# A row of inverse roots sent to all partitions through DRAM instead of by transposes

## The chip, the core and the metric

The kernel runs on one core of a Trainium2 chip. The metric is the device time of one execution in microseconds, as the median of several runs. The core has five engines that run their own instruction streams: TensorE (PE, matmuls and transposes), VectorE (DVE), ScalarE (ACT), GpSimd (POOL) and SyncE (SP, which issues most DMAs; ACT issues the others). Every stream is worked off in order, and an instruction that has to wait holds back all that stand behind it in its stream.

## The reference

One decoder layer over 2048 tokens of width 1024. `h = RMSNorm(x)` is projected by one wide matrix, the result is cut into three branches (an RWKV-7 time mixing, a sliding-window attention, a cross-attention), each branch is gated and projected back, the three are merged by sigmoid gates, and the merged row is projected by `w_out` and added to `x`. The change touches the first line alone:

```
def rms_norm(x, g):
    xf = x.astype(jnp.float32)
    y = xf * lax.rsqrt(jnp.mean(xf * xf, axis=-1, keepdims=True) + RMS_EPS)
    return (y * g.astype(jnp.float32)).astype(x.dtype)
...
h = rms_norm(x, norm_g[l])
p = h @ w_in[l]
```

## The kernel before

The tokens are worked off in four superblocks of 512 (`TB`). Activations lie transposed, channels on the partitions and 512 tokens along the row, and every float32 product is made of three matmuls on a high and a low half (`gemm3`, L534 to L536; in the output product L1334 to L1336). So `h` of a superblock is eight pairs of tiles `hH`, `hL` of 128 x 512.

To scale `x` by its inverse root, the kernel needs one factor for each token, as a row of 512, the same on all 128 partitions. The sums of squares come the other way, with tokens on partitions. While superblock `sb` is worked on, `x_sums(sb + 1, ss)` (L1350) loads eight blocks of the next tokens through ACT's DMA queue and squares and sums them on ACT. `x_scales(sb + 1, ss)` (L1360) adds the two halves on DVE (L1366, tile `rs`, 128 x 4), takes the power -0.5 on POOL (`rpow`, L489 and L491), spreads each column over 128 columns on DVE (`bcast_T`, L572), transposes the four 128 x 128 pieces on PE (L574) into a PSUM tile `as_`, and copies that on ACT (L1371) to the tile `rb`, which is one of the six buffers `rt`. `x_cols` (L1374) loads eight blocks of the transposed `x` through ACT's DMA queue (L1380), multiplies each by `rb` on DVE (L1383), and splits it into `hH` (ACT, L1385) and `hL` (DVE, L1386).

This stands at the end of each of the first three superblocks, here called the first, second and third end (at about 520, 1041 and 1561 us of the profile). At that place PE works on eight merges (`merge(0, ...)`, twelve matmuls each, into one of two PSUM tiles `mm`), and then on the output product (`output`, L1327), which begins at about 531.6, 1052.6 and 1573.5 us. A merge's PSUM tile is read by DVE at L1317, the result is added at L1318, and `split_acc` splits it (ACT L1322, DVE L1324). The output product fills four PSUM tiles: the first `mm`, `as_`, the second `mm`, `as_`. Its first `mm` is the tile of the seventh merge, its second that of the eighth, so each waits for that merge's L1317.

The weights come as blocks of 128 x 512 in high and low halves, tile `whl`, seven buffers (`WR`). A block is either loaded as `raw` (L514, three buffers) and split on ACT (L515) and DVE (L516), sometimes kept in DRAM for later (L520), or read back from there (L511). All of these DMAs stand in SP's stream.

The order within the streams is not that of the code. `order` (L310) gives all instructions to `lay_out` (L196), which plays the program through with costs from a table (`cost_PE` and so on) and fixes every engine's order. A plain DMA counts 2200 ns there (`cost_SP`, L142). What is planned later, by the framework, are the semaphores: the DMAs of SP and ACT share eight of them, DMAHW0 to DMAHW7, in turn, and a DMA that is to count on one of them first waits, in its own engine's stream, until the DMA that last used it has landed.

Of the kernel before, what the change touches and what calls it, by code (L numbers as in the profile page):

```python
# [9 lines left out]
F32 = mybir.dt.float32  # L10
# [10 lines left out]
TB = 512  # L21
# [297 lines left out]
def build(tc, A, nsb=4):  # L319
    nc = tc.nc  # L320
# [3 lines left out]
    def pool(name, bufs, **kw):  # L324
        return es.enter_context(tc.tile_pool(name=name, bufs=bufs, **kw))
# [24 lines left out]
    def s_ps():  # L350
        return ps.tile([128, 512], F32, name="as_", bufs=2)
# [43 lines left out]
    def tmp(tag="rt", bufs=NRT):  # L395
        return rp.tile([128, TB], F32, name=tag, bufs=bufs)
# [55 lines left out]
    def pcol(name, i=0):  # L452
        o, w = PV[name]
        return pv[:, o + i:o + i + 1]
# [13 lines left out]
    def dcol(name, i=0):  # L468
        return dv[:, DV[name][0] + i:DV[name][0] + i + 1]
# [14 lines left out]
    def rpow(out, in_, add, scale=1.0):  # L484

        if scale == 1.0:
            G.tensor_scalar(out, in_, add, None, op0=ALU.add)  # L487
        else:
            G.tensor_scalar(out, in_, scale, add, op0=ALU.mult, op1=ALU.add)  # L489
        n = out.shape[-1]  # L490
        G.tensor_tensor(out, out, mhalf[:, :n], op=ALU.pow)  # L491


    dp = pool("dp", 1, space=bass.MemoryType.DRAM)
# [44 lines left out]
    def proj(blk, hT, n=TB):  # L539
        o = mm_ps()  # L540
        gemm3(o[:, :n], [(w, (hT[0][:, k, :n], hT[1][:, k, :n])) for k, w in enumerate(wtiles(A["w_in"][blk], 8, ("in", blk)))])
        return o
# [25 lines left out]
    def bcast_T(out, st, nh, ntile):  # L568

        w = 128 // nh  # L570
        rep = tmp()[:, :ntile * 128]
        V.tensor_copy(rep.rearrange("p (a b) -> p a b", b=w), st[:, :ntile * nh].unsqueeze(2).to_broadcast([128, ntile * nh, w]))  # L572
        for i in range(ntile):
            PE.transpose(out[:, i * 128:(i + 1) * 128], rep[:, i * 128:(i + 1) * 128], ident)  # L574
# [69 lines left out]
    def row_sums(rows):  # L644

        ss = xp.tile([128, 4, 2], F32, name="ss", bufs=2)
        for i, xr in enumerate(rows):
            sq = rp.tile([128, 512], BF16, name="ibc", bufs=2)
            if i % 2:
                V.tensor_tensor_reduce(sq, xr, xr, 1.0, 0.0, ALU.mult, ALU.add, ss[:, i // 2, 1:])  # L650
            else:
                S.activation(sq, xr, AF.Square, accum_out=ss[:, i // 2, :1])
        rs = xp.tile([128, 4], F32, name="rs", bufs=2)
        n = len(rows) // 2
        V.tensor_tensor(rs[:, :n], ss[:, :n, 0], ss[:, :n, 1], op=ALU.add)
        return rs
# [80 lines left out]
    def shift(o, blk, mu, omu, sb, tag, bufs=1, t=None):  # L737
        t = rp.tile([128, TB], F32, name=tag, bufs=bufs) if t is None else t
        S.activation(t, o, AF.Copy, scale=omu)
        V.scalar_tensor_tensor(t[:, 1:], o[:, :TB - 1], mu, t[:, 1:], op0=ALU.mult, op1=ALU.add)  # L740
        V.scalar_tensor_tensor(t[:, 0:1], carry[sb % 2][:, blk:blk + 1], mu, t[:, 0:1], op0=ALU.mult, op1=ALU.add)
        V.tensor_copy(carry[1 - sb % 2][:, blk:blk + 1], o[:, TB - 1:TB])  # L742
        return t
# [6 lines left out]
    def park(sb):  # L750

        return [[dp.tile([4, 128, 4, 2, 128], F32, name=f"{n}{sb}_{u}") for u in range(2)] for n in ("fq", "fb")] + \
            [[dp.tile([4, 64, 4, 2, C], F32, name=f"fv{sb}_{u}") for u in range(2)]]
# [307 lines left out]
    def split_y(y, yh, yl, br, j, sb):  # L1061
        a = yp.tile([128, TB], F32R, name="yh")
        b = yp.tile([128, TB], F32R, name="yl")
        S.activation(a, y, AF.Copy)
        V.tensor_tensor(b, y, a.bitcast(F32), op=ALU.subtract)  # L1065
        yh.append(a)
        yl.append(b)
# [231 lines left out]
    def gate(i, o, hT):  # L1299
        gp = proj(B_G + 8 * i + o, hT)  # L1300
        t = gp_.tile([128, TB], F32, name="gt", bufs=2) if i else g2()
        S.activation(t, gp, AF.Tanh, scale=0.5)  # L1302
        return t
# [46 lines left out]
    def x_sums(sb, ss):  # L1350

        for i in range(4):
            for u in range(2):
                yield 45
                xr = gp_.tile([128, 512], F32, name="sx", bufs=1)
                load = nc.scalar.dma_start(xr, A["x"][sb * TB + i * 128:sb * TB + (i + 1) * 128, u * 512:(u + 1) * 512])
                manual[load.ins.name] = [newest[0]]
                S.activation(xr, xr, AF.Square, accum_out=ss[:, i, u:u + 1])

    def x_scales(sb, ss=None):  # L1360

        if not sb:
            rs = row_sums(x0)
        else:
            rs = xp.tile([128, 4], F32, name="rs", bufs=2)
            V.tensor_tensor(rs, ss[:, :, 0], ss[:, :, 1], op=ALU.add)  # L1366
        rpow(rs, rs, EPS, 1.0 / D)
        bc = s_ps()
        bcast_T(bc, rs, 1, 4)
        rb = tmp()  # L1370
        S.activation(rb, bc, AF.Copy)  # L1371
        return rb
# [17 lines left out]
    for i, _ in enumerate(mem_kv(mT)):  # L1390
        if i == AT1:
            rb = x_scales(0)
# [3 lines left out]
    for sb in range(nsb):  # L1396
        wa = proj(B_WA, hT)
        low = shift(wa, B_WA, pcol("mu_wa"), dcol("omu_wa"), sb, "rr_")
        S.activation(low[EV], low[EV], AF.Tanh)

        lwla = [rp.tile([128, TB], F32R, name=f"lwla{i}") for i in range(2)]
        for t, h, o in zip(lwla, (EV, OD), (OD, EV)):
            S.activation(t[h], low[h], AF.Copy)
            V.tensor_tensor(t[o], low[h], t[h].bitcast(F32), op=ALU.subtract)
        yas = []
        ya, yb, yc_ = ([], []), ([], []), ([], [])
        accs = []

        def stream_r():
            parks = park(sb)  # L1410
            dk = xp.tile([128, 4, NC_], F32, name="dk", bufs=1)
            Pl = xp.tile([128, 4, NC_], F32, name="Pl", bufs=1)
            yts = []
            for p0 in (0, 2):
                group = []
                fn, fy = (dp.tile([4, 2, NC_, 32, 32], F32, name=f"{n}{sb}_{p0}") for n in ("fn", "fy"))
                for p in (p0, p0 + 1):
                    yield from rwkv_prep(p, p - p0, parks, dk, Pl, fn, sb, hT, lwla, group)
                yield from rwkv_inverse(group, parks, fn, fy)
                yts += [g[2] for g in group]  # L1420
            yield from rwkv_chain(parks, dk, Pl, hT, yts, yas)
            yield 0.412

        def stream_f():
            for h in range(4):
                yield from cross_head(h, sb, hT, *yc_)
            if not sb:
                rope_tables(0)
            yield from swa_kv(sb, hT)
            yield 6.938  # L1430
            for j in range(4):
                yield from weave(swa_pair(j, sb, hT, *yb), merge(2, *yc_, accs, hT, first=True, orange=(2 * j, 2 * j + 1)))
            yield from merge(1, *yb, accs, hT)
            for o in range(8):
                gates.append(gate(0, o, hT))
                yield 5.908

        gates = []
        ss = xp.tile([128, 4, 2], F32, name="ss", bufs=2)
        streams = [paced(g, PACE[min(sb, 1)][i]) for i, g in enumerate((stream_r(), stream_f()))]  # L1440
        if sb + 1 < nsb:
            streams.append(x_sums(sb + 1, ss))
        for _ in weave(*streams):
            pass
        for p in range(4):
            split_y(yas[p], *ya, "a", p, sb)
        rb = None
        if sb + 1 < nsb:
            rope_tables(sb + 1)
            rb = x_scales(sb + 1, ss)  # L1450
        parts = []
        for o in range(8):
            for _ in merge(0, *ya, accs, hT, gates=gates, orange=(o,)):
                pass
            parts.append(split_acc(accs[o]))
        if rb is not None:
            hT = x_cols(sb + 1, rb)
        output(sb, *zip(*parts))
# [4 lines left out]
def paced(g, paces):  # L1463

    for f, d in zip(paces, g):
        yield f * d


def weave(*gens):

    live = [[0.0, i, g] for i, g in enumerate(gens)]
    now = 0.0
    while live:
        live.sort(key=lambda x: x[:2])
        e = live[0]
        try:
            d = next(e[2])
        except StopIteration:
            live.pop(0)
            continue  # L1480
        e[0] += d
        t = min(x[0] for x in live)
        if t > now:
            yield t - now
            now = t
# [64 lines left out]
```

## Time and profile before

| what | value |
|---|---|
| median of 3 runs | 2143.12 us (2143.11 to 2143.8) |
| the profiled execution's own time | 2143.2 us |
| its span, first to last instruction | 2141.4 us |
| PE busy | 2125.9 us, 14260 matmuls and transposes |
| DVE, ACT, POOL busy | 1418.5, 802.1, 133.6 us |
| mean granted TensorE clock | 1.000 |
| DMA | 519.17 MB, mean 242 GB/s |

In rows of the timeline the first number is the start in us of the span, the second the duration in us; then come the engine, the line, the operation and what it writes and reads. SPq and ACTq are DMAs issued by these engines, and their duration is the time of the issue, not of the transfer. In rows by line and window, "DMA to landing" is the time from the start of the issue to the last piece's arrival. A matmul of 512 columns shows about 0.39 us but follows the one before it after some 0.23 us, as they are pipelined.

### The profile page before, as it was taken

Reading aid. Unit: us, or ns where it says so; the run is one execution under the profiler, and the core shown is the slowest. Engines: PE = TensorE matmul, PEld = TensorE weight load, DVE = VectorE, ACT = ScalarE, POOL = GpSimd, SP = SyncE. Lnnn points to the kernel's source line nnn. Section 1 sums busy time; section 2 is a strip of 40 time slices with the busy share of each in tenths; the row PEclk is TensorE's granted clock in tenths of the full one; section 3 lists DMA queues with packets and bytes.
Section 4 is the critical chain, followed back from the end, with each engine's and each line's share of the span. In section 5 each row is a group of like instructions: output and inputs, shape, how many; then the busy total and the mean of one; then the engine's idle time right before and its main releaser. Section 6 shows DMA issues by size and latency. Waiting matters only on the chain.

```text
span 2141.4 us, 37426 instructions
## 1 busy us (share of the span) xinstructions
PE 2125.9 (99%) x14260; PEld 1753.8 (82%) x14260; DVE 1418.5 (66%) x3234; ACT 802.1 (37%) x1699; POOL 133.6 (6%) x180
## 2 busy tenths in 40 slices
PE   9999999999999999999999999999999999999999
PEld 7888887778888888878888888887888888888787
DVE  7879888468576787546647778736455777873532
ACT  7655554326344353303424434420423334331220
POOL 1001000001001000001000000000100010000000
PEclk9999999999999999999999999999999999999999
DMA  9988888987866678695876667777676676768665
GB/s 331 364 282 271 272 289 283 340 294 251 285 203 205 192 218 239 198 311 193 281 254 211 201 180 228 236 231 260 216 264 220 197 204 199 233 186 269 217 206 181
DMA packets 308594, 519.17 MB, mean 242 GB/s; under 512 B 89280, under 2 KB 175552, under 8 KB 308416
## 3 DMA queue, kind: packets, MB, share of 16 engines
q1 hardware_dynamic: 292288, 487.42, 70.9%
q10 hardware_dynamic: 16128, 29.37, 4.2%
q8 instruction: 113, 1.85, 0.4%
q14 instruction: 65, 0.53, 0.1%
HBM read 378.80 MB, written 137.89 MB: 241 GB/s over the span
## 4 chain that ended last, share of the span: by engine, by line
PE 91%; DVE 4%; DMA 3%; ACT 1%; issue 1%; POOL 0%; SPq 0%; ACTq 0%; DVEq 0%; POOLq 0%
PE mm L534 23%; PE mm L535 23%; PE mm L536 23%; PE mm L1334 1%; PE mm L1336 1%; PE mm L1335 1%; DMA raw<-in_w_in 1%; PE rw L1016 1%; PE rw L999 1%; PE oo L1283 1%; DVE whl L516 1%; PE rw L831 1%; PE rw L850 1%; DMA k<-whl 1%; PE oo L831 1%
## 5 line engine op out<-in xcount | busy, mean ns | idle before, releaser
L534 PE MATMUL mm<-hH,whl 128*128 128x512 f32 x1888 | 745.2, 395 | 2.0 <-DVE carry L742 1.4
L535 PE MATMUL mm<-hL,whl 128*128 128x512 f32 x1888 | 743.5, 394 | 0.0
L536 PE MATMUL mm<-hH,whl 128*128 128x512 f32 x1888 | 742.5, 393 | 0.0
L534 PEld LDWEIGHTS mm<-hH,whl 128*128 128x128 f32 x1888 | 354.8, 188 | 74.4 <-ACT whl L515 1.8
L536 PEld LDWEIGHTS mm<-hH,whl 128*128 128x128 f32 x1888 | 354.7, 188 | 71.4
L535 PEld LDWEIGHTS mm<-hL,whl 128*128 128x128 f32 x1888 | 355.0, 188 | 70.1 <-DVE hL L1386 0.2
L515 ACT ACTIVATE whl<-raw 128x512 fp32r<-128x512 f32 x174 | 109.1, 630 | 186.4 <-PE mm L536 131.7
L516 DVE TENSOR_TENSOR whl<-raw,whl 128x512 fp32r<-128x512 f32 x174 | 119.2, 687 | 61.7 <-ACT whl L515 55.7
L534 PE MATMUL mm<-yh,whl 128*128 128x512 f32 x384 | 151.4, 394 | 1.3 <-DVE gt L1317 1.2
L535 PE MATMUL mm<-yl,whl 128*128 128x512 f32 x384 | 150.3, 391 | 0.0
L536 PE MATMUL mm<-yh,whl 128*128 128x512 f32 x384 | 149.7, 390 | 0.0
L1302 ACT ACTIVATE gt<-mm 128x512 f32<-128x512 f32 x64 | 37.8, 590 | 179.3 <-PE mm L536 179.0
L534 PEld LDWEIGHTS mm<-yh,whl 128*128 128x128 f32 x384 | 72.1, 188 | 17.2 <-DVE gt L1317 1.6
L1317 DVE SCALAR_TENSOR_TENSOR gt<-gt,mm 128x512 f32<-128x512 f32 x32 | 21.9, 686 | 95.5 <-PE mm L536 95.3
L535 PEld LDWEIGHTS mm<-yl,whl 128*128 128x128 f32 x384 | 72.1, 188 | 15.0 <-DVE yl L1065 0.5
L536 PEld LDWEIGHTS mm<-yh,whl 128*128 128x128 f32 x384 | 72.1, 188 | 14.7
L487 POOL TENSOR_SCALAR st<-st 128x4 f32<-128x4 f32 (+1 forms) x32 | 12.7, 397 | 1019.7 <-DVE st L1093 418.8
L1341 DVE SCALAR_TENSOR_TENSOR ya<-mm,ya 128x512 f32<-128x512 f32 x16 | 11.0, 689 | 93.8 <-PE mm L1336 93.8
L1251 ACT ACTIVATE g<-g,mxs,st 128x128 f32<-128x128 f32 x128 | 61.6, 484 | 28.1 <-DVE mxs L1244 28.1
L892 DVE TENSOR_TENSOR ibc<-km,Yi 128x126 f32<-128x126 f32 (+22 forms) x248 | 62.9, 254 | 7.7 <-DMA km<-fn 2.1
L893 DVE TENSOR_TENSOR Yi<-Yi,ibc 128x126 f32<-128x126 f32 (+22 forms) x248 | 62.7, 253 | 5.6
L491 POOL TENSOR_TENSOR st<-st,mhalf 128x8 f32<-128x8 f32 (+1 forms) x36 | 52.7, 1463 | 3.0
(1828 smaller groups left out, 3579.5 us busy)
## 6 DMA issues: line engine op xcount, KB each, us to landing
whl<-k SPq DMA_DIRECT2D x474, 512.0 KB, 4.2
k<-whl SPq DMA_DIRECT2D x162, 512.0 KB, 4.8
raw<-in_w_in SPq DMA_DIRECT2D x118, 256.0 KB, 4.2
fq<-big SPq DMA_DIRECT2D x64, 256.0 KB, 4.4
fb<-big SPq DMA_DIRECT2D x64, 256.0 KB, 4.3
big<-fq SPq DMA_DIRECT2D x32, 512.0 KB, 6.4
big<-fb SPq DMA_DIRECT2D x32, 512.0 KB, 5.6
ya<-in_x ACTq DMA_DIRECT2D x32, 256.0 KB, 4.7
```

Source lines behind the costliest of these rows:

```text
L491: G.tensor_tensor(out, out, mhalf[:, :n], op=ALU.pow)
L515: S.activation(w[:, 0], raw, AF.Copy)
L516: V.tensor_tensor(w[:, 1], raw, w[:, 0].bitcast(F32), op=ALU.subtract)
L534: PE.matmul(out, lh, rh, start=i == 0, stop=False)
L535: PE.matmul(out, lh, rl, start=False, stop=False)
L536: newest[0] = PE.matmul(out, ll, rh, start=False, stop=i == n - 1).ins.name
L831: m = PE.matmul(g[:, c], BK[h, c0 + c], Q[h, c0 + c], start=True, stop=True)
L892: V.tensor_tensor(bc[:, :m, :w], Nb[:, s, s + 1:].unsqueeze(1).to_broadcast([128, m, w]), B[:, :m, s:s + 1].to_broadcast([128, m, w]), op= ...
L893: V.tensor_tensor(B[:, :m, s + 1:], B[:, :m, s + 1:], bc[:, :m, :w], op=ALU.add)
L1251: S.activation(P_, P_, AF.Exp, scale=r2[:, b, i:i + 1], bias=mx[:, b, i:i + 1], accum_out=mx[:, b, 2 + i:3 + i])
L1302: S.activation(t, gp, AF.Tanh, scale=0.5)
L1317: V.scalar_tensor_tensor(g, g, 1.0, pp, op0=ALU.add, op1=ALU.mult)
```

## The change

For the second to the fourth superblock, `x_scales` now ends after the power. It writes the 128 x 4 tile `rs` to a row of 512 numbers in DRAM (tile `xr`, one for each superblock), so that each partition's four numbers go to four places 128 numbers apart: 512 pieces of 4 bytes. It is called by the third of the woven streams, right after the last sum of squares. After `rope_tables`, one DMA reads the row back to all 128 partitions of an `rt` buffer (128 pieces of 2 KB). The spreading on DVE (L572), the four transposes (L574) and ACT's copy (L1371) are gone at the three ends; the first superblock keeps them. Both new DMAs are in SP's stream.

```
         rpow(rs, rs, EPS, 1.0 / D)
+        if sb:
+            row = dp.tile([1, TB], F32, name=f"xr{sb}")
+            nc.sync.dma_start(row[0].rearrange("(i t) -> t i", t=128), rs)
+            return row
         bc = s_ps()
...
+        rows = []
+
+        def stream_x():
+            yield from x_sums(sb + 1, ss)
+            rows.append(x_scales(sb + 1, ss))
+
         if sb + 1 < nsb:
-            streams.append(x_sums(sb + 1, ss))
+            streams.append(stream_x())
...
             rope_tables(sb + 1)
-            rb = x_scales(sb + 1, ss)
+            rb = tmp()
+            nc.sync.dma_start(rb, rows[0].to_broadcast([128, TB]))
```

In the changed file the lines below L1367 stand 4 lower up to the streams and 10 lower after the reading DMA's place: L1380, L1383, L1385 and L1386 of before are L1384, L1387, L1389 and L1390, the write is L1370, the read L1461. The planner orders the new program anew; PE, DVE, ACT and SP differ from before at the three ends only.

SP's stream at the second end, changed kernel, with the semaphores that each instruction waits for (`DMAHW` and a number: that semaphore's last DMA; the first name in a DMA's row is mostly the semaphore that it counts on itself):

```order
L511 DMA whl_11453<-k143_6205 128x1024 [waits DMAHW7_49,PE_49]
L1370 DMA xr2_11140<-rs_11136 128x4x1 [waits DMAHW0_49,Pool_49]
L514 DMA raw_11587<-in_w_out 128x512 [waits DMAHW1_49,DVE_49]
L1461 DMA rt_11184<-xr2_11140 128x512 [waits DMAHW2_49,DMAHW0_49]
L520 DMA k155_11472<-whl_11467 128x1024 [waits DMAHW4_49]
L511 DMA whl_11486<-k144_6241 128x1024 [waits DMAHW7_49,PE_49]
```

The write counts on DMAHW0, a load of `w_out` behind it on DMAHW1, and the read waits for the write by DMAHW0. Before, L511, L514, L520 and L511 followed each other there.

ACT's stream at the same place, before:

```order
L515 ACTIVATE whl_11477<-raw_11478 128x512 [waits DMAHW3_49,DMAHW4_49,DMAHW0_49,PE_49]
L1371 ACTIVATE rt_11194<-as__11187 128x512 [waits PE_49]
L1380 DMA rt_11386<-in_xt 128x512
L1380 DMA rt_11391<-in_xt 128x512 [waits DMAHW0_49]
L1380 DMA rt_11396<-in_xt 128x512 [waits DMAHW2_49]
L1322 ACTIVATE g2_11307<-mB_8942 128x512 [waits DVE_49]
L1380 DMA rt_11401<-in_xt 128x512 [waits DMAHW4_49]
L1380 DMA rt_11406<-in_xt 128x512 [waits DMAHW5_49]
L1322 ACTIVATE g2_11333<-mB_9093 128x512 [waits DVE_49]
```

and in the changed kernel:

```order
L515 ACTIVATE whl_11467<-raw_11468 128x512 [waits DMAHW5_49,DMAHW6_49,DMAHW2_49,PE_49]
L1384 DMA rt_11376<-in_xt 128x512 [waits DMAHW3_49]
L1384 DMA rt_11381<-in_xt 128x512 [waits DMAHW5_49]
L1384 DMA rt_11386<-in_xt 128x512 [waits DMAHW6_49]
L1384 DMA rt_11391<-in_xt 128x512 [waits DMAHW0_49]
L1384 DMA rt_11396<-in_xt 128x512 [waits DMAHW1_49]
L1322 ACTIVATE g2_11297<-mB_8937 128x512 [waits DVE_49]
L1322 ACTIVATE g2_11323<-mB_9088 128x512 [waits DVE_49]
```

All five loads of `xt` now stand ahead of both splits L1322. The fourth waits for DMAHW0, whose last DMA is the write of the row, and the fifth for DMAHW1, whose last DMA is the load of `raw_11587` in SP's rows above. Before, the five waited for DMAs issued by 1041.44 us: the fifth for the `whl` load of that time.

DVE's stream at the second end, changed kernel (`mm_11308`, `mm_11329` and `mm_11355` are the sixth, seventh and eighth merge):

```order
L1317 SCALAR_TENSOR_TENSOR g2_11069<-g2_11069,mm_11308 128x512 [waits PE_49]
L1324 TENSOR_TENSOR mB_11299<-mB_8937,g2_11297 128x512 [waits Activation_49]
L1318 TENSOR_TENSOR mB_9088<-mB_9088,g2_11069 128x512 [waits DVE_49]
L1324 TENSOR_TENSOR mB_11325<-mB_9088,g2_11323 128x512 [waits Activation_49]
L1317 SCALAR_TENSOR_TENSOR g2_11100<-g2_11100,mm_11329 128x512 [waits PE_49]
L516 TENSOR_TENSOR whl_11500<-raw_11501,whl_11500 128x512 [waits DMAHW2_49,DMAHW1_49,Activation_49]
L1318 TENSOR_TENSOR mB_9455<-mB_9455,g2_11100 128x512 [waits DVE_49]
L1387 TENSOR_TENSOR rt_11376<-rt_11376,rt_11184 128x512 [waits DMAHW3_49,DMAHW2_49]
L1317 SCALAR_TENSOR_TENSOR g2_11131<-g2_11131,mm_11355 128x512 [waits PE_49]
```

The first multiplication of `x` (L1387) waits for the row by DMAHW2, and stands four instructions later than before, just ahead of the eighth merge's L1317.

DVE's stream at the third end, changed kernel (`mm_16525`, `mm_16546` and `mm_16567` are the sixth, seventh and eighth merge):

```order
L1318 TENSOR_TENSOR mB_14320<-mB_14320,g2_16301 128x512 [waits DVE_49]
L1387 TENSOR_TENSOR rt_16588<-rt_16588,rt_16416 128x512 [waits DMAHW4_49,DMAHW3_49]
L1317 SCALAR_TENSOR_TENSOR g2_16332<-g2_16332,mm_16546 128x512 [waits PE_49]
L1324 TENSOR_TENSOR mB_16542<-mB_14320,g2_16540 128x512 [waits Activation_49]
L1318 TENSOR_TENSOR mB_14687<-mB_14687,g2_16332 128x512 [waits DVE_49]
L1390 SCALAR_TENSOR_TENSOR hL_16587<-rt_16588,c_pv_105,hH_16586 128x512 [waits Activation_49]
L1387 TENSOR_TENSOR rt_16593<-rt_16593,rt_16416 128x512 [waits DMAHW5_49]
L1317 SCALAR_TENSOR_TENSOR g2_16363<-g2_16363,mm_16567 128x512 [waits PE_49]
```

Here the first L1387 waits for the row by DMAHW3 and stands one instruction later than before, ahead of the seventh and the eighth merge's L1317. On PE, the output product's second `mm` begins eight matmuls after its first at the second end and nine at the third.

## Prediction

> **What bounds the kernel now.** I read the page's engine rows and the chain that ended last, then the timeline of each engine around the three ends, then the landings of the DMAs there. The page says that PE is never idle to speak of, and that the chain runs through its matmuls:
>
> ```profile
> PE 2125.9 (99%) x14260; PEld 1753.8 (82%) x14260; DVE 1418.5 (66%) x3234; ACT 802.1 (37%) x1699; POOL 133.6 (6%) x180
> PE 91%; DVE 4%; DMA 3%; ACT 1%; issue 1%; POOL 0%; SPq 0%; ACTq 0%; DVEq 0%; POOLq 0%
> ```
>
> So work taken from PE shortens the kernel by what it held PE up, and a new wait costs only what reaches PE. The profiled execution took 2143.2 us, against a median of 2143.12, so I add differences to 2143.2 as they are. From no change a measurement can tell about 0.2%, that is 4.3 us: the limits are 2138.8 and 2147.4.
>
> **What the transposes cost on PE.** The timeline of PE, at the third, the first and the second end (in this order):
>
> ```profile
> 1555.83 0.39 PE L536 MATMUL mm<-yh,whl 128*128 128x512 f32 x1
> ...
> 1563.99 0.39 PE L536 MATMUL mm<-yh,whl 128*128 128x512 f32 x1
> 1564.22 0.60 PE L574 MATMUL as__16424<-c_ident,rt 128*128 128x128 f32 x4
> ...
> 1567.20 0.39 PE L536 MATMUL mm<-yh,whl 128*128 128x512 f32 x1
> ```
> ```profile
> 523.21 0.39 PE L536 MATMUL mm<-yh,whl 128*128 128x512 f32 x1
> ...
> 527.31 0.39 PE L536 MATMUL mm<-yh,whl 128*128 128x512 f32 x1
> ```
> ```profile
> 1044.15 0.39 PE L535 MATMUL mm<-yl,whl 128*128 128x512 f32 x1
> ...
> 1047.59 0.39 PE L536 MATMUL mm<-yh,whl 128*128 128x512 f32 x1
> ```
>
> Undisturbed, 36 steps lie between the first two rows: 8.16 / 36 = 0.227 us a matmul. From 1563.99 to 1567.20 there are 12 matmuls, so 2.72 us were due and 3.21 passed: 0.49 us for the transposes. At the first end 15 matmuls took 4.10 us for 3.40 (0.70), at the second 13 took 3.44 for 2.95 (0.49). Sum: a gain of 1.7 us, sure as far as the rows go; the DVE spreading and ACT's copy stood in the shadow of this busy PE and give nothing by themselves. That is all that the change can gain, so "faster by over 0.2%" has hardly a way.
>
> **When the row comes back.** The power is done on POOL, and only then can SP issue the write; the read waits for the landing. The trace has no write of 4-byte pieces; the nearest rows are the smallest parked writes, and for the read the broadcast of the positions, which has the same shape:
>
> ```profile
> 521.55 1.01 POOL L491 TENSOR_TENSOR rs<-rs,mhalf 128x4 f32<-128x4 f32 x1
> ```
> ```profile
> fn<-big SPq DMA_DIRECT2D x64, 32.0 KB, 4.0
> rt<-in_positions SPq DMA_DIRECT2D x4, 256.0 KB, 4.8
> ```
> ```profile
> 537.76 1.28 DVE L1383 TENSOR_TENSOR rt<-rt 128x512 f32<-128x512 f32 x2
> ```
>
> First end: 522.6 + 4.0 + 4.8 = 531.4, while DVE comes to the first multiplication at 537.76. Six us of cover, so nothing is lost. (The cover is the same for SP: what stands behind the waiting read are weight loads whose block is used six blocks of 2.72 us later; a wait of 4 us there reaches nobody.)
>
> **Second end: ACT is held by a shared semaphore.** The five loads of `xt` now stand ahead of the split L1322, and the fifth waits for the landing of the `w_out` load that SP issues at 1046.3. The rows of before, of DVE, ACT, that load with its landing, and PE where the output product starts:
>
> ```profile
> 1045.62 0.68 DVE L516 TENSOR_TENSOR whl<-raw,whl 128x512 fp32r<-128x512 f32 x1
> ...
> 1048.09 0.69 DVE L1324 TENSOR_TENSOR mB<-mB,g 128x512 fp32r<-128x512 f32 x1
> 1048.70 0.68 DVE L1318 TENSOR_TENSOR mB<-mB,g 128x512 f32<-128x512 f32 x1
> 1049.30 1.29 DVE L1383 TENSOR_TENSOR rt<-rt 128x512 f32<-128x512 f32 x2
> 1050.51 0.68 DVE L1317 SCALAR_TENSOR_TENSOR g<-g,mm 128x512 f32<-128x512 f32 x1
> ```
> ```profile
> 1045.03 2.35 ACTq L1380 DMA_DIRECT2D rt<-in_xt  x3
> 1047.43 0.63 ACT L1322 ACTIVATE g<-mB 128x512 fp32r<-128x512 f32 x1 [1.81 <-DVE mB L1318]
> ```
> ```profile
> L514 SPq DMA_DIRECT2D raw<-in_w_out x1: 332/332/332, 1046.3 to 1046.3; - x1
> ...
> DMA to landing us min/median/max: 5.2/5.2/5.2
> ```
> ```profile
> 1052.58 0.39 PE L1334 MATMUL mm<-whl,g 128*128 128x512 f32 x1
> ```
>
> ACT does stop for its DMAs: the three issues end at 1047.38 and L1322 starts at 1047.43. The load cannot go earlier, since L516, which frees its buffer, ends at 1046.30 as before. It landed 5.2 us later; loads of this kind take a median of
>
> ```profile
> raw<-in_w_out SPq DMA_DIRECT2D x24, 256.0 KB, 3.4
> ```
>
> so it lands between 1049.7 and 1051.5. I take the middle, 1050.6, since three of the five `xt` loads now start about 0.7 us sooner (ACT's copy no longer stands ahead of them) and two come later. With 0.4 us for the fifth issue, L1322 starts at S = 1051.0 instead of 1047.43. Behind it DVE must do L1324, L1318, wait for ACT's second L1322, then L1324 and the seventh merge's L1317: with 0.63 on ACT and 0.60 from one DVE start to the next (1048.70 to 1049.30), L1317 ends at S + 3.95. PE would be ready for the output product at 1052.58 - 0.49 = 1052.09 and starts at 1055.0. The eighth merge's L1317 stands four DVE steps later and ends at S + 6.35 = 1057.35; PE asks for that tile eight matmuls on, at 1056.8, so 0.55 is added. The sum is S + 4.55 - 1052.09 = 3.5 us, between 2.6 and 4.4.
>
> **Third end: DVE is held by the row.** The rows of before:
>
> ```profile
> 1561.51 1.01 POOL L491 TENSOR_TENSOR rs<-rs,mhalf 128x4 f32<-128x4 f32 x1
> ```
> ```profile
> 1568.31 0.69 DVE L1317 SCALAR_TENSOR_TENSOR g<-g,mm 128x512 f32<-128x512 f32 x1
> 1568.92 0.69 DVE L1383 TENSOR_TENSOR rt<-rt 128x512 f32<-128x512 f32 x1
> ```
> ```profile
> L511 SPq DMA_DIRECT2D whl<-k x1: 319/319/319, 1562.4 to 1562.4; - x1
> ...
> DMA to landing us min/median/max: 3.2/3.2/3.2
> ```
> ```profile
> L511 SPq DMA_DIRECT2D whl<-k x1: 319/319/319, 1565.6 to 1565.6; - x1
> ...
> DMA to landing us min/median/max: 6.3/6.3/6.3
> ```
> ```profile
> L511 SPq DMA_DIRECT2D whl<-k x1: 320/320/320, 1568.3 to 1568.3; - x1
> ...
> DMA to landing us min/median/max: 6.5/6.5/6.5
> ```
> ```profile
> 1573.55 0.39 PE L1334 MATMUL mm<-whl,g 128*128 128x512 f32 x1
> ```
>
> The write goes out at 1562.7, right behind the load that lands at 1565.6, so I let it land at about 1566.4 (3.7 us; the median write above takes 4.0). The read follows the next weight load in SP's queue, and the `xt` loads run beside both. That weight load lands at 1571.9 - 0.5 = 1571.4, the one after it at 1574.8 - 0.5 = 1574.3; the row, half as large as a weight block, falls in the first half between: 1571.4 to 1572.9. I take R = 1572.2. The lower bound is 1566.6 plus an undisturbed 3.2, or 1569.8. From R on, DVE runs L1387, the seventh merge's L1317, L1324, L1318, L1390, L1387 and the eighth's L1317, which ends at R + 4.4; PE wants its tile nine matmuls after 1573.55 - 0.49 = 1573.06, at 1575.1. The loss is R - 1570.7: 1.5 us, between 0 and 2.2. (ACT's fifth `xt` issue waits here for the write itself; that is the write's 1566.4, early enough for the seventh merge, so PE doesn't feel it.)
>
> **Sum.** -1.7 + 3.5 + 1.5 = +3.3 us: 2146.5 us, no change that can be told, on the slow side. With the bounds of the two waits: 2144.1 to 2148.1.
>
> **A rule about small pieces and the fixed cost of a DMA.** The Trainium skill, "DMA: Bandwidth & Descriptors", section "Anatomy of one DMA", puts a DMA's fixed cost at about 2.0 us; by it both legs at the third end would take about 4.6 us, an estimate, and the row would be there before DVE asks. This trace disagrees, with 3.2 us for an undisturbed load, 4.0 for a small write and 6.3 beside the `xt` loads.
>
> **The rivals.**
>
> *Everything is hidden* (chance 0.14). Both legs take as long as the undisturbed load of 3.2 us, and the `w_out` load lands before ACT has issued the first four: then only the transposes' 1.7 us count, 2141.5 us. For it: the planner counts 2.2 us a DMA and found no wait. Against it: 5.2, 6.3 and 6.5 us in just these places. The Trainium skill's 2.0 us above would lead here.
>
> *The write of 512 pieces lands late* (chance 0.28), the case that ends slower. Place: SP's stream at the second and third end. The pieces go out ahead of the `w_out` load in the same queue, so d us more for them push that load, ACT's fifth `xt` issue and S back by d, and at the third end R too. Price: 2d on top of 3.3, so 2148.5 us for d = 1 and 2150.5 for d = 2; from d = 0.5 on it is slower by over 0.2%. For it: no row shows pieces so small, and there are 512 where `fn` has 256. Against it: `fn` lands in the time of far larger transfers, so pieces seem to cost little. The Trainium skill, "DMA: Bandwidth & Descriptors", section "Rules for kernel authors", speaks against such a write: a last dimension that is not contiguous becomes one descriptor for each element.
>
> *PE slows after the pause* (chance 0.08). The first matmuls of the program run at half pace, and the longest pause inside it does not bring this back:
>
> ```profile
> 2.38 5.49 PE L383 MATMUL oo<-onesw 128*128 128x512 f32 x12 [2.38 <-ACT onesw L380]
> ...
> 7.66 0.41 PE L534 MATMUL mm<-mB,whl 128*128 128x256 f32 x1
> ```
> ```profile
> 414.27 0.46 PE L1008 MATMUL rw<-W,big 64*64 64x64 f32 x16 [1.58 <-DMA big<-fb]
> ...
> 415.23 0.40 PE L535 MATMUL mm<-hL,whl 128*128 128x512 f32 x1
> 415.46 0.40 PE L536 MATMUL mm<-hH,whl 128*128 128x512 f32 x1
> ```
>
> Twelve took 7.66 - 2.38 = 5.28 us where 2.72 is usual: 2.6 us more. After 1.58 us of pause the step is 0.23. A pause of 2.9 us at the second end lies between the two; if it is enough, the time is 2146.5 + 2.6 = 2149.1 us. The Trainium skill, "TensorE: Matmul & The Clock Gate", section "Part 1: The HAM clock gate", has the array fall to half rate after an idle window of about 3.4 us; by that rule 2.9 us is just too short, and the trace's 1.58 agrees as far as it goes.
>
> **How the numbers follow.** The forecast has 0.50, of which about 0.10 lies over 2147.4 by its own bounds. Slower: 0.10, the late write's 0.25 with d over 0.5, and the slow PE's 0.08, together 0.43. Faster by over 0.2%: 0.02, since only 1.7 us are there to gain. Within: the rest, 0.55. The range goes from the hidden case (2141.3) to the late write with d = 1.6 (2149.8), and leaves out about one in ten.
>
> **What would show it.** In the new profile: no L574 at the three ends and steps of 0.23 there; at the second end ACT's L1322 at about 1051 right behind five ACTq issues, and PE's first L1334 waiting for DVE's L1317 by about 2.9 us; at the third end DVE idle ahead of L1387 until about 1572, by the DMA of the row, and PE held some 1.5 us in two short waits. The first end shows no wait. The prediction is wrong if PE waits at neither end (the landings were sooner), or if the write takes more than 4.5 us.

## The result, and the profile after

The changed kernel takes 2173.6 us (median of 4 runs, 2172.42 to 2174.95) against 2143.46 us (4 runs, 2143.11 to 2143.92): 1.0141 times as long, 95% interval 1.0129 to 1.0153. It is 30 us slower; the forecast was 3.3 us slower, with a range up to 2149.8. The profiled execution took 2172.42 us, with a span of 2170.6, 29.2 more than before.

The page's engine row and chain:

```profile
PE 2132.4 (98%) x14248; PEld 1756.8 (81%) x14248; DVE 1418.4 (65%) x3231; ACT 801.3 (37%) x1696; POOL 136.4 (6%) x180
PE 84%; DMA 6%; DVE 6%; ACT 2%; issue 1%; SPq 0%; POOL 0%; ACTq 0%; DVEq 0%
```

The twelve transposes are gone, yet PE is busy 6.5 us longer, and PE's share of the chain has fallen from 91 to 84%, with more on DMA and DVE. The new write, with the time from its issue to its landing, and then the read:

```profile
L1370 SPq DMA_DIRECT2D xr<-rs x3: 371/377/386, 520.6 to 1581.3; - x3
...
DMA to landing us min/median/max: 10.8/11.5/11.9
```
```profile
L1461 SPq DMA_DIRECT2D rt<-xr x3: 319/320/326, 532.6 to 1592.9; - x3
...
DMA to landing us min/median/max: 5.4/6.0/6.5
```

The read takes about what it was given (4.8 us at the first end, 5.8 at the third). The write takes three times as long, for 2 KB. And it is not alone in being late. The same 7.2 us of the second end, in the changed kernel and before (length, busy time of each engine with its instructions, granted clock, share of the DMA engines that is busy, GB/s):

```profile
1052.00:1059.20 7.20, 5.97 (x27) 4.62 (x25) 1.26 (x3) 0.00 (x0) 0.00 (x0) 1.00 0.77 85
```
```profile
1052.00:1059.20 7.20, 7.20 (x34) 5.95 (x33) 7.20 (x13) 2.51 (x4) 0.00 (x0) 1.00 1.01 362
```

While the write is under way the DMA engines are still shown three quarters busy, but they move 85 GB/s in place of 362. None of the transfers issued in that time lands before the write does, and all of them land within 6 us behind it. The stops of PE, at the first, the second and the third end:

```profile
536.86 0.80 PE L1334 MATMUL mm<-whl,g 128*128 128x512 f32 x1 [6.31 <-DVE g L1317]
...
537.88 0.63 PE L1336 MATMUL mm<-whl,mB 128*128 128x512 f32 x1
538.31 0.63 PE L1335 MATMUL as__6163<-whl,g 128*128 128x512 f32 x1
```
```profile
1068.47 0.77 PE L1334 MATMUL mm<-whl,g 128*128 128x512 f32 x1 [10.49 <-ACT whl L515]
```
```profile
1595.25 0.79 PE L534 MATMUL mm<-yh,whl 128*128 128x512 f32 x1 [6.20 <-DVE g L1317]
```

Behind each stop the matmuls follow each other by 0.43 us (537.88 to 538.31) in place of 0.23, for some ten of them; the granted clock of the stretch from 1066 to 1075 us is 0.56, where it was 1.00 before the stop. With two small stops at the third end, the stops add 25.0 us to the steps of PE and the slow matmuls 7.3 (0.6 before); less the 1.7 us of the transposes that is 30.0, against 29.2 of span.

Who waited for what, by the list of waits (engine and line, what ended the wait, total us, times, longest) in the windows of the first, the second and the third end:

```profile
ACT whl L515 <- DMA raw<-in_w_out: 13.2, 3, 7.4
DVE whl L516 <- ACT whl L515: 8.0, 2, 6.0
...
PE mm L1334 <- DVE g L1317: 6.3, 1, 6.3
```
```profile
ACT g L1322 <- DMA rt<-in_xt: 13.8, 1, 13.8
```
```profile
ACT g L1322 <- DMA rt<-in_xt: 10.2, 1, 10.2
...
DVE rt L1387 <- DMA rt<-xr: 3.4, 1, 3.4
```

At the first end it is not the row that is waited for, but a block of `w_out` whose load stands behind the write: it was issued at 521.13 and landed 12.07 us later, ACT cannot split it (L515), DVE stands at its L516, and the seventh merge's L1317 is queued behind that. At the second and third end ACT stands at an issue of `xt`. For the second end, the timelines of SP, ACT and DVE:

```profile
1048.32 0.37 SPq L1370 DMA_DIRECT2D xr<-rs  x1
1052.06 0.33 SPq L514 DMA_DIRECT2D raw<-in_w_out  x1
1059.12 0.32 SPq L1461 DMA_DIRECT2D rt<-xr  x1
```
```profile
1050.24 14.14 ACTq L1384 DMA_DIRECT2D rt<-in_xt  x4
1064.43 0.63 ACT L1322 ACTIVATE g<-mB 128x512 fp32r<-128x512 f32 x1 [13.80 <-DMA rt<-in_xt]
```
```profile
1067.69 0.68 DVE L1317 SCALAR_TENSOR_TENSOR g<-g,mm 128x512 f32<-128x512 f32 x1
```

The last four of the five issues take 14.14 us: the fourth load goes out at 1059.12, the moment the write has landed (1059.11), the fifth at 1064.05, when the `w_out` load issued at 1052.06 has (1064.03). These are the two semaphores named under "The change", the second of which the prediction counted on; they were only held much longer. The profile puts PE's wait down to L515, but that ended at 1067.56; the seventh merge's L1317, in the row of DVE, ended at 1068.37, just before PE went on at 1068.47.

At the third end the fifth issue of `xt` waits for the write itself (landed at 1592.82). ACT's L1322 behind it starts at 1593.25, DVE's L1324 and the sixth merge's L1317 follow, and PE goes on at 1595.25. The row is waited for only after that, and costs PE no more than the two small stops of 0.47 and 0.73 us.

### The profile page after: what moved, and what is told of

The parts are those of the page before. It is cut to its first block, busy times and chain, and to the rows that moved or that the text cites. A ratio compares the mean times of both kernels' runs of the same rounds, so it can differ in the third digit from the quotient of the medians.

```text
span 2170.6 us, 37411 instructions
## 1 busy us (share of the span) xinstructions
PE 2132.4 (98%) x14248; PEld 1756.8 (81%) x14248; DVE 1418.4 (65%) x3231; ACT 801.3 (37%) x1696; POOL 136.4 (6%) x180
## 4 chain that ended last, share of the span: by engine, by line
PE 84%; DMA 6%; DVE 6%; ACT 2%; issue 1%; SPq 0%; POOL 0%; ACTq 0%; DVEq 0%
PE mm L534 21%; PE mm L535 20%; PE mm L536 20%; PE mm L1334 1%; PE mm L1336 1%; PE mm L1335 1%; DVE whl L516 1%; DMA raw<-in_w_out 1%; PE rw L1016 1%; DMA raw<-in_w_in 1%; PE rw L999 1%; PE oo L1283 1%; PE rw L831 1%; DMA k<-whl 1%; PE rw L850 1%
## 5 line engine op out<-in xcount | busy, mean ns | idle before, releaser
L515 ACT ACTIVATE whl<-raw 128x512 fp32r<-128x512 f32 x174 | 109.4, 630 | 196.6 <-PE mm L536 137.4
L516 DVE TENSOR_TENSOR whl<-raw,whl 128x512 fp32r<-128x512 f32 x174 | 119.4, 688 | 70.4 <-ACT whl L515 64.0
L1302 ACT ACTIVATE gt<-mm 128x512 f32<-128x512 f32 x64 | 37.8, 590 | 177.9 <-PE mm L536 177.7
L1317 DVE SCALAR_TENSOR_TENSOR gt<-gt,mm 128x512 f32<-128x512 f32 x32 | 22.0, 688 | 96.4 <-PE mm L536 96.3
L487 POOL TENSOR_SCALAR st<-st 128x4 f32<-128x4 f32 (+1 forms) x32 | 12.7, 398 | 1046.5 <-DVE st L1093 449.2
L1334 PE MATMUL mm<-whl,g 128*128 128x512 f32 x128 | 51.4, 401 | 18.0 <-ACT whl L515 10.5
```

Source lines behind the costliest of these rows:

```text
L515: S.activation(w[:, 0], raw, AF.Copy)
L516: V.tensor_tensor(w[:, 1], raw, w[:, 0].bitcast(F32), op=ALU.subtract)
L1317: V.scalar_tensor_tensor(g, g, 1.0, pp, op0=ALU.add, op1=ALU.mult)
L1334: PE.matmul(op[tt], mh[k][:, tk], wh, start=k == 0, stop=False)
```

## The experiments

Theory A: the write of 512 pieces of 4 bytes is slow by itself and holds every transfer behind it. Theory B: it is the path that costs, that is the order of ACT's and DVE's streams, the shared semaphores and the round trip, and the write looks slow because of the other traffic. Each kernel is compared with runs of the kernel before on the same chip, whose medians were 2143.27, 2142.94 and 2144.26 us.

### The write by itself

A small kernel issues one write, two loads of 256 KB right behind it, and waits for all three.

> A small kernel of its own that computes nothing of the reference (its output is zeros): eight forms of write to DRAM from SP, each three times, each with two loads of 256 KB right behind it (one from SP, one from ACT), everything waited for before the next. Forms: none; 512 pieces of 4 bytes as in the change (p4); 128 of 4 bytes (p4one); 1024 of 4 bytes (p4two); 512 of 4 bytes, each 128 bytes from the next (p4far); 128 of 16 bytes (p16); 512 of 64 bytes (p64); 512 of 512 bytes (p512). Theory A (each small piece costs memory time, and all transfers behind wait for it): p4 lands after 10 to 12 us as in the changed kernel and both loads behind it are as late; p4one and p16 land after 4 to 5 us, p4two after about 20; if the size of the piece counts, p64 and p512 land in 3 to 6 us, if only the number counts, p64 takes 10 to 12 too; if it is the crowding of pieces in few lines of memory, p4far is fast. Theory B (the landings of the changed kernel were late because of the other transfers beside them, not of the pieces): all forms land within 2 us of each other, p4 after 3 to 5 us.

The zero writes of its output ran beside the first forms, so only the later ones can be read. p4far, 512 pieces of 4 bytes 128 bytes apart, landed after 2.0 to 3.3 us; p16 after 1.4 to 3.4, p64 after 1.8 to 3.4, p512 after 2.3 to 3.8. Small pieces alone are not slow. The next kernel had the output written last, and varied the distance:

```
+            row = dp.tile([1, 512, step], F32, name=f"{form.__name__}_{n}")
+            nc.sync.dma_start(row[0, :, 0].rearrange("(i t) -> t i", t=128), rs[:, :4])
```

> A small kernel of its own that computes nothing of the reference (its output is zeros), in the manner of the first one, the loads behind each write now undisturbed: 512 pieces of 4 bytes whose places in DRAM are 4, 8, 16, 32 or 64 bytes apart (apart_four to apart_sixtyfour), 256 adjacent pieces of 8 bytes (pairs), 128 of 16 (fours), 128 of 32 (eights), and a load of 512 pieces of 4 bytes from DRAM (fetch). Theory A1 (writes into the same 64 bytes of memory wait for each other, about 0.55 us each): the landing falls with the number of pieces in 64 bytes: about 10 us for 16 (apart_four), 5 to 6 for 8 (apart_eight, pairs), 2.5 to 3.5 for 4, under 3 for 2 and 1; fetch is fast. Theory A2 (only adjacent pieces hurt, or only those under 8 bytes): apart_eight already lands within 3 us, or pairs does. For both the two loads behind apart_four land as late as the write, 9 to 13 us, against 3 to 5 behind none.

Its DMAs by tile (times three, KB each, median us to landing); of the loads the first is one with no write ahead of it, the second one behind apart_four:

```profile
a__71<-in_x SPq DMA_DIRECT2D x1, 256.0 KB, 3.0
...
a__85<-in_x SPq DMA_DIRECT2D x1, 256.0 KB, 12.7
...
apart_four<-rs SPq DMA_DIRECT2D x3, 2.0 KB, 9.7
apart_eight<-rs SPq DMA_DIRECT2D x3, 2.0 KB, 4.0
apart_sixteen<-rs SPq DMA_DIRECT2D x3, 2.0 KB, 3.0
...
apart_sixtyfour<-rs SPq DMA_DIRECT2D x3, 2.0 KB, 2.3
pairs<-rs SPq DMA_DIRECT2D x3, 2.0 KB, 3.5
fours<-rs SPq DMA_DIRECT2D x3, 2.0 KB, 1.4
```

The same 512 pieces cost 9.7 us when they touch and 2.3 us when they lie 64 bytes apart, and the load behind them is late by as much (12.7 against 3.0). The load of 512 such pieces (fetch) took 3.2 us, so reading them is not slow. That is theory A: the write is slow by itself, when its pieces lie close to each other in memory. Neither form of it gave the right curve: at 8 bytes 5 to 6 us or under 3 were expected, and 4.0 were measured. Then the number:

> A small kernel of its own that computes nothing of the reference (its output is zeros), in the manner of the second one: adjacent pieces of 4 bytes, always 16 to 64 bytes of DRAM, in rising number: 16 (line_one), 32 (line_two), 128 (line_eight), 256 (line_sixteen), 512 (line_thirtytwo, the write of the change), 1024 (line_sixtyfour) and 2048 (line_many). If pieces within the same 64 bytes wait for each other and other pieces do not, the extra time is nearly the same for all of them: 8 to 12 us landings from 16 pieces to 2048. If each piece has its price (512 cost about 8 us more than a plain write), 16 and 32 land within 2.5 us, 128 after 4, 256 after 6, 1024 after 18, 2048 after 34.

```profile
line_one<-rs SPq DMA_DIRECT2D x3, 0.1 KB, 1.3
line_two<-rs SPq DMA_DIRECT2D x3, 0.1 KB, 4.2
line_eight<-rs SPq DMA_DIRECT2D x3, 0.5 KB, 8.0
...
line_thirtytwo<-rs SPq DMA_DIRECT2D x3, 2.0 KB, 9.4
...
line_many<-rs SPq DMA_DIRECT2D x3, 8.0 KB, 12.7
```

From 128 pieces on (8.0 us) the number hardly counts: 2048 take 12.7. So there is no price for each piece. But 16 pieces in one stretch of 64 bytes land after 1.3 us (the loads behind them take 4.4 in place of 3.0) and 32 after 4.2, so "within 64 bytes" isn't right either. Why close pieces are slow, and within what stretch of memory, stays open.

### The same program with larger pieces

```
-                load = nc.scalar.dma_start(xr, A["x"][sb * TB + i * 128:sb * TB + (i + 1) * 128, u * 512:(u + 1) * 512])
+                load = nc.scalar.dma_start(xr, A["x"][sb * TB:(sb + 1) * TB].rearrange("(t i) d -> i t d", i=4)[i, :, u * 512:(u + 1) * 512])
...
-            nc.sync.dma_start(row[0].rearrange("(i t) -> t i", t=128), rs)
+            nc.sync.dma_start(row[0].rearrange("(t i) -> t i", i=4), rs)
```

> The changed kernel, but the sums of squares take every fourth token to a partition, so that each partition's four numbers lie together in the row: 128 pieces of 16 bytes in place of 512 of 4. All streams keep the order of the changed kernel. Theory A (pieces): the write lands in 4 to 6 us in place of 10.8 to 11.9, and the time falls by 20 to 28 us, to 2145 to 2153. Theory B (the path: the shared semaphores, the order of ACT's and DVE's streams, the round trip): nothing of this is changed, 2170 to 2176.

2149.75 us, ratio 1.0033 (1.0023 to 1.0043): with every stream in the order of the changed kernel, three quarters of the loss are gone, as theory A expected. The profiled execution took 2152.94 us, 3.2 more than the median, so its stops may be larger than usual. The write, and PE at the third end:

```profile
L1370 SPq DMA_DIRECT2D xr<-rs x3: 319/326/382, 521.9 to 1567.9; - x3
...
DMA to landing us min/median/max: 2.6/4.3/6.2
```
```profile
1581.67 0.47 PE L1334 MATMUL mm<-whl,g 128*128 128x512 f32 x1 [3.16 <-issue]
...
1582.46 0.63 PE L1334 MATMUL as__16629<-whl,g 128*128 128x512 f32 x1
1582.89 0.63 PE L1335 MATMUL as__16629<-whl,g 128*128 128x512 f32 x1
```

This is the kernel that the forecast described: a write of about 4 us (2.6, 6.2 and 4.3 at the three ends). PE stops nowhere at the first end, 3.40 us at the second and 3.16 at the third, and slow matmuls follow both stops (0.43 us from 1582.46 to 1582.89).

### One part alone

The write in the kernel before, read by nobody, and all other instructions in their old order:

```
         rpow(rs, rs, EPS, 1.0 / D)
+        if sb:
+            row = dp.tile([1, TB], F32, name=f"xr{sb}")
+            nc.sync.dma_start(row[0].rearrange("(i t) -> t i", t=128), rs)
         bc = s_ps()
```

> The kernel before, with the transposes, and the 512-piece write of the row added, which nobody reads. All other instructions keep the order of before. Theory A: the write lands after 10 to 12 us and holds every load issued in that time, so PE stops at the ends although nobody waits for the row: 2155 to 2175. Theory B: nobody waits for it, so 2143 to 2144.

2160.59 us, ratio 1.0081 (1.0066 to 1.0096): 17 us for a write that is not used, as theory A expected. PE stops 3.74 us at the first end, 2.41 and 0.50 at the second and 6.19 at the third. The stop of 2.41 us tells something of PE's pace after a pause:

```profile
1058.82 0.47 PE L1334 MATMUL mm<-whl,g 128*128 128x512 f32 x1 [2.41 <-ACT whl L515]
1059.13 0.40 PE L1335 MATMUL mm<-whl,g 128*128 128x512 f32 x1
1059.36 0.40 PE L1336 MATMUL mm<-whl,mB 128*128 128x512 f32 x1
```

After 2.41 us PE goes on at 0.23 us a step; after 3.16 us and more slow matmuls come. The other half, the changed kernel with the read but without the write:

```
-            nc.sync.dma_start(rb, rows[0].to_broadcast([128, TB]))
+            behind(nc.sync.dma_start(rb, A["w_proj"][0, 0, :1].to_broadcast([128, TB])), rows[0], done=True)
```

> The changed kernel without the write: the broadcast read takes 512 numbers of an input in place of the row, once the power is done, so x is scaled by wrong factors. The planner orders the three ends a little differently. Theory A: without the write there is the gain of 1.7 us and little loss, 2141 to 2146. Theory B (the order of the streams and the wait for the read): the waits stay, 2155 or more.

2144.08 us, ratio 1.0003 (0.9994 to 1.0013): no change that can be told. PE's stops are 0.47 us at the second end and 1.00 and 0.36 at the third. The planner gave this kernel other streams than the changed kernel has (at the second end the five loads of `xt` go out some 14 us before the output product, against some 8 before it was due in the changed kernel). So it shows that a row can be read without loss, and not what the read costs in the order of the changed kernel.

### The order of the streams

The same slow write, but the planner is told how long the two DMAs take:

```
         self.dur, self.busy = 4200 if parked else 2200, 420
+        if any(r[0].startswith("xr") for r in self.writes):
+            self.dur = 11500
+        if any(r[0].startswith("xr") for r in self.reads):
+            self.dur = 6000
```

> The changed kernel, but the planner counts 11.5 us for the write of the row and 6 us for its read, in place of 2.2 each, so it plans the streams of the three ends by the durations that the profile showed. Theory A (the write holds all transfers behind it): what the order cost beside that goes, the held loads stay: 2152 to 2164, near the write alone. Theory B (the order of the streams is what made it slow): 2146 or less.

2143.71 us, ratio 1.0003 (0.9994 to 1.0012). Here theory A, which counted on 2152 at least, fails, and theory B's 2146 or less holds, though the write is as slow as ever. The write's landings, and ACT at the second end (the code's lines stand 4 lower here, so L1326 is L1322, L1388 is L1384):

```profile
L1374 SPq DMA_DIRECT2D xr<-rs x3: 377/378/385, 521.0 to 1562.2; - x3
...
DMA to landing us min/median/max: 9.7/10.2/11.2
```
```profile
1052.30 0.63 ACT L1326 ACTIVATE g<-mB 128x512 fp32r<-128x512 f32 x1 [1.93 <-DVE mB L1322]
1052.51 7.14 ACTq L1388 DMA_DIRECT2D rt<-in_xt  x5
1059.69 0.63 ACT L1326 ACTIVATE g<-mB 128x512 fp32r<-128x512 f32 x1 [6.76 <-DMA raw<-in_w_out]
```

ACT still stands for 7 us at the issues of `xt`, but now they come after the split at 1052.30, when PE has already begun the output product (1052.26), and PE does not stop at the second end at all. The weight blocks are also still late, but blocks loaded ahead cover that. So the slow write makes everything behind it late, and it is the order that decides whether PE waits. With larger pieces and this very order:

> The streams of the kernel whose planner counts 11.5 and 6 us for the row's two DMAs, all in the same order, but pieces of 16 bytes, so the write is fast. What is still lost there by the slow write comes off, and the transposes are gone: theory A and theory B both 2141 to 2143; a time of 2143.7 again would say that the slow write costs nothing in that order.

2140.04 us, ratio 0.998 (0.9972 to 0.9989): faster than both kernels, and 1 us below the times expected. Matched matmul by matmul with before, it gains 0.42, 0.49 and 0.49 us on PE at the three ends, which is the transposes; the rest of the 0.2% lies in small differences elsewhere or isn't explained. In the order of this kernel the slow write still cost about 1.0003 / 0.998 = 0.23% (5 us; matched matmul by matmul, the two profiles show 3 of them at the three ends). With the durations that fit the larger pieces (5000 and 7000 in the lines above):

> Pieces of 16 bytes, and the planner counts 5 us for the write and 7 for the read, about what the run with pieces of 16 bytes showed. If durations that fit are enough to lose the waits of that run (3.4 and 3.2 us of PE), 2141 to 2143; if not, 2144 to 2150.

2141.59 us, ratio 0.999 (0.9981 to 0.9999): the waits of the first run with these pieces (3.40 and 3.16 us) are gone, as expected if fitting durations are enough; one stop of 0.63 us is left near the ends, in the output product of the first.

### Two ways that did not help

The sums of squares paced at 40 in place of 45, with the large and with the small pieces:

> The changed kernel with pieces of 16 bytes and with the sums of squares paced at 40 in place of 45, so that the row stands in DRAM well before the end of the superblock. Theory A: no slow write, and no wait for the row; the transposes' 1.7 us are gained if the loads of xt hold nobody: 2141 to 2144. Theory B (path and order): 2146 or more.

> The changed kernel with its 512 pieces of 4 bytes, only the sums of squares paced at 40 in place of 45, so that the write is issued well before the end of the superblock. Theory A: the write still takes 10 to 12 us and still holds the loads behind it, but they may be ahead of need there: 2142 to 2150 if the weight buffers cover it, 2155 to 2170 if they don't. Theory B (waits for the row alone): the row is there long before, 2141 to 2144.

2155.2 us (1.0053, 1.0039 to 1.0067) and 2175.16 us (1.0148, 1.0134 to 1.0162). With the large pieces theory A counted on 2141 to 2144 and misses, and the time lies where theory B put it; with the small ones the time lies above what either gave. The row is early, but the planner then puts the reads, the loads of `xt` and `x_cols` earlier too, among the merges, and other instructions now stand behind them. For the small pieces, the longest of PE's waits in the whole program:

```profile
PE mm L534 <- ACT g L1302: 21.6, 3, 10.7
```

ACT's L1302, which reads a gate's PSUM tile `mm` and so clears it, now comes too late at all three ends; at the first, DVE waits 8.6 us for the load of the positions behind the write. Last, the loads of `xt` issued by POOL:

```
-                nc.scalar.dma_start(xt, A["xt"][k * 128:(k + 1) * 128, sb * TB:(sb + 1) * TB])
+                nc.gpsimd.dma_start(xt, A["xt"][k * 128:(k + 1) * 128, sb * TB:(sb + 1) * TB])
```

> The changed kernel with its 512 pieces of 4 bytes and the planner's old durations, only the loads of xt issued by POOL in place of ACT, so that ACT's stream has no issue that waits for a landing. Theory C (the slow write hurts at the second and third end because ACT stands at an issue of xt, which waits on a semaphore for the write or for a load behind it, with L1322 and L515 behind): the stops of PE at these two ends shrink to under 3 us each, the first end's 6 stays: 2150 to 2160. Rival D (the weight blocks that are held behind the write are late by themselves): the stops stay, 2165 to 2178.

2172.22 us, ratio 1.0132 (1.0117 to 1.0148). The time is in rival D's range, but not by its mechanism. The waits at the second end:

```profile
DVE rt L1387 <- DMA rt<-xr: 7.9, 1, 7.9
...
PE mm L1334 <- DVE g L1317: 7.1, 1, 7.1
```

ACT is free, and PE waits all the same: now DVE stands at L1387 until the row is there (7.9 us, and 9.5 at the third end), with the eighth merge's L1317 behind it. Theory C named one of two waits that lie side by side, each of 8 us and more.

## Why the prediction was wrong

- **The step that failed** is the write's duration: "I let it land at about 1566.4 (3.7 us; the median write above takes 4.0)". It lands after 10.8 to 11.9 us, far over the 4.5 us that the forecast gave as a sign of being wrong. The bound came from `fn`, 256 pieces of 128 bytes, and the reason from the number of pieces ("there are 512 where `fn` has 256"). The number was the wrong measure: 128 pieces of 4 bytes that touch take 8.0 us, 512 that lie apart 2.3. The Trainium skill's rule in "DMA: Bandwidth & Descriptors", section "Rules for kernel authors", one descriptor for each element, pointed at the right instruction, but descriptors are not what it costs: four times fewer elements cost nearly the same.
- **The late write** was the right rival with a wrong size: it was worked out for d up to 2 us, and d was 7 to 8. Its price of 2d on 3.3, with d = 7.1 at the second end (10.8 - 3.7), gives +17.5 us. What is missing up to 30 are two things that the rival left out: the first end (its stop adds 6.5) and the slow PE (7.3); with them it is 31.3. That the sum comes so close is in part luck, for at the third end the loss took another way than by the row. The forecast let ACT's fifth issue of `xt` pass there ("PE doesn't feel it"), since the write would land at 1566.4; that issue held ACT's L1322 for 10.2 us and gave the stop of 6.20 us, while DVE waited 3.4 us for the row.
- **The first end**: "a wait of 4 us there reaches nobody" failed, since it was not SP that was held but all transfers. The row itself came at 538.0, about when DVE had wanted it; a `w_out` block behind the write came 12 us after its issue and stopped PE for 6.31 us.
- **PE's pace after a pause** got a chance of 0.08 and happened at all three ends, 2.3 to 2.7 us each; 2.6 had been worked out. It was made to hang on one pause of 2.9 us, and the pauses were 6 to 10. The bracket from the runs is 2.41 us (no slow matmul) and 3.16 us (slow ones) of idle time as the trace shows it, or 2.80 and 3.55 us from start to start. The Trainium skill's window of about 3.4 us in "TensorE: Matmul & The Clock Gate", section "Part 1: The HAM clock gate", lies in the second bracket and just above the first.
- **Right** were the transposes' worth (0.49 us each at the second and third end, as forecast, and 0.42 for 0.70 at the first, in the kernel that has no other loss there), the two semaphores that hold ACT, and both chains of waits, as the run with pieces of 16 bytes shows. At the second end there, ACT's L1322 starts at 1050.64 (1051.0 in the forecast) and PE's output product at 1054.69 (1055.0). The loss of 3.5 us that was forecast came as one stop of 3.40 us in place of 2.9 and 0.55, partly by luck: PE got there 1 us sooner, and its slow matmuls hid the second wait. The third end was given 1.5 us, at most 2.2, and took 3.16 there, by the wait for the row as forecast: from the write's issue (1567.87) to the row's landing (1580.26) 12.4 us passed where 9.5 had been worked out, since the read alone took 8.05 beside the loads of `xt`. (The range's lower end, 2141.3, is 0.2 below what the hidden case gives, 2143.2 - 1.7; this changes nothing.)
- **The fixed cost** of 2.0 us, by which everything would have been hidden, was no guide. The Trainium skill gives it, in "DMA: Bandwidth & Descriptors", section "Anatomy of one DMA", which the prediction names, for DMAs issued by GpSimd. SP issues both legs here, and a write of 512 values, issued alone, landed after 1.4 us as 16-byte pieces and after 9.7 as adjacent 4-byte ones.
- **The theory formed on the result** (the held loads alone would stop PE) fell too: with the streams in another order the same slow write cost 0.23%. Shown is that both are needed for the 30 us, the slow write and the order of the streams in the changed kernel. That what matters in this order are the splits and L1317 behind things that wait for the write is read from the traces; no run moved these alone. Larger pieces in the old order took some 24 us off (6.5 slower than before are left of 30), the other order with the old pieces 29.

## What to carry to other kernels

When a DMA writes to DRAM, look first at how small its pieces are and how close together they land: 128 and more pieces of 4 bytes side by side, each from another partition than its neighbours, took 8 to 13 us here and made the loads behind them 7 to 10 us late, while the same 512 values as 16 bytes from each partition took 1.4 us. Choose the mapping of data to partitions so that what one partition holds lies together. And where a planner sets the order, give it the duration that the trace shows for each new DMA: here a wrong 2.2 us for each leg turned a transfer that could be covered into 30 us.

## What was not expected of the hardware

- A write of 2 KB in adjacent 4-byte pieces lands after 9.1 to 11.9 us, and loads of 256 KB issued right behind it by either engine land after 11 to 13 in place of 3. In the kernel the DMA engines are then shown as 77% busy and move 85 GB/s in place of 362. Reading such pieces takes 3.2 us.
- The price falls with the distance of the pieces (9.7, 4.0, 3.0, 2.2, 2.3 us at 4, 8, 16, 32, 64 bytes) and hardly rises with their number from 128 (8.0) to 2048 (12.7); 16 take 1.3. The cause, in the memory or in the DMA engines, is not settled by these runs.
- After a stop of 3.16 us PE ran its first three matmuls at full pace and only then eight at about half pace, so the slowing came behind the pause.
